# 512-column products for the output projection, the second MLP matrix and the values, with a shared pool of weight buffers

## The chip, the cores and the metric

The kernel runs on one core of one Trainium2 chip. The metric is the device time of one execution in microseconds; each kernel is executed several times and the median is taken. TensorE (PE) multiplies and writes only to PSUM, VectorE (DVE) and ScalarE (ACT) work on SBUF and PSUM, SyncE (SP) starts the transfers, GpSimd (POOL) has little to do here.

## The reference, cut to what matters

Two layers. In each, a mixer with four branches (gated convolution, Conformer convolution module, differential attention, neighbourhood attention) is followed by gates, one output projection and a squared-ReLU MLP. Layer 0 works on 256 latent and 256 context tokens, layer 1 on the 256 latent tokens alone, with keys and values of the context.

```python
glu = p[I_CA] * jax.nn.sigmoid(p[I_CG])
y_b = jax.nn.silu(layer_norm(dwconv(glu, dw, db), lg, lb))       # norm over 512 channels
...
o = jnp.einsum('bhqk,bkhv->bqhv', pd, v)                          # values v: 512 columns per branch
...
y = merge_out(p[I_GATE], (y_a, y_b, y_c, y_d), w_branch[l], b_branch[l], w_o[l])   # merged @ w_o
x = layer_norm(DEEPNORM_ALPHA * x + g1 * y, ln_g[l, 0], ln_b[l, 0])
a = relu(h @ w1); y = (a * a) @ w2                                # w1: 1024 x 4096, w2: 4096 x 1024
x = layer_norm(DEEPNORM_ALPHA * x + g2 * y, ln_g[l, 1], ln_b[l, 1])
```

All numbers are float32. To keep that precision, both operands of a large product are split into a high and a low float32r part, and a product is three matmuls: high by high, high by low, low by high.

## The kernel before, in words

Weights come from memory in units of 128x1024 floats (512 KB): a DMA on SP brings `raw`, ACT rounds it to `whi`, DVE subtracts to `wlo`, PE uses both. `weight_order()` lists the units, `w_load`, `w_hi` and `w_lo` walk down the list, and `weight()` hands the next unit to the main thread. Each of the three stages has three buffers. A further two hold `araw`, the blocks of the adaLN matrix; DVE (and ACT for a few) multiplies these into the running sums `sums`, from which one small matmul makes the modulation row. That work fills the stretches from about 300 to 530 us and from 660 to 950 us.

Every thread of work is a Python generator. A planner (`Sched.run`) knows costs per instruction and a priority per thread, and at each step gives out the instruction that can start first; this sets the order on each engine, and the engines then run those orders with semaphores between them. On PE, the main thread (projections, merge, MLP) and the attention threads interleave in this way.

Projections `in`, `br` and `f1` compute their results with channels on partitions and tokens along the columns (512 columns in layer 0, 256 in layer 1). The value projections (`values`, units `dv` and `nv`), the output projection (`out_proj`, `wo`) and the second MLP matrix (`ff2`, `f2`, shown as `f` in the profile) have 128 tokens on partitions and weights along the columns: 256 columns per PSUM tile, `nb` counting the four column blocks, a unit holding four of the eight 128-row slices of one block. PSUM has eight buffers of one bank; at most four are `main` (projections), four `att` (attention).

`residual` works off a PSUM tile on DVE: a multiplication by the gate row, an addition, a `bn_stats`. `ff2_evac` adds up the four quarters of the MLP in `yacc`. `conv_b_norm` computes the mean (`mu`) and variance (`var`) over 512 channels, which lie in four tiles of 128 partitions, by matmuls with a matrix of constants in float32. In the last layer `blocks` takes the last two column blocks tile by tile, so that the first token tile can be normalised while the second is computed; two units are kept (`held`) for the second pass.

Of the kernel before, what the change touches and what calls it, by code (L numbers as in the profile page):

```python
# [21 lines left out]
N_S = 70  # L22
# [19 lines left out]
MARGIN = 20  # L42
CAPS_PS = {"main": 4, "att": 4, "ada": 1}
# [11 lines left out]
def unit_table():  # L55

    names = []
    for m in range(76):
        if not (M_DV <= m < M_DV + 4 or M_NV <= m < M_NV + 4):
            names.append(("in", m))  # L60
    for br in ("dv", "nv"):
        names += [(br, s, h) for s in range(2) for h in range(2)]
    names += [("br", i, mp) for i in range(4) for mp in range(4)]
    names += [("wo", nb, h) for nb in range(4) for h in range(2)]
    names += [("f1", m) for m in range(32)]
    names += [("f2", qd, nb, h) for qd in range(4) for nb in range(4) for h in range(2)]
    return {n: i for i, n in enumerate(names)}
# [237 lines left out]
class Kernel(Sched):  # L305
    def __init__(self, tc, es, aps):
# [125 lines left out]
    def gemm(self, out, pairs, cost):  # L432

        n = len(pairs)
        step = max(1, int(1300 // (3 * cost)))
        for i in range(0, n, step):
            calls, r = [], []
            for j in range(i, min(n, i + step)):
                a, b = pairs[j]
                calls += self.mm3(out, a, b, j == 0, j == n - 1)  # L440
                r += [a[0], a[1], b[0], b[1]]
            yield self.mm(calls, [out], r, (cost + 2) * len(calls))

# [108 lines left out]
    def w_load(self):  # L552
        for i, (l, name) in enumerate(self.order):
            if i < FIRST:
                yield self.wait("x0", 1, W_AFTER[i])
            raw = yield self.alloc("raw", name="raw")
# [3 lines left out]
    def w_hi(self):  # L560
        for i in range(len(self.order)):
# [6 lines left out]
            else:  # L568
                hi = yield self.alloc("whi", dt=F32R, name="whi", n=1)
# [3 lines left out]
    def w_lo(self):  # L573
        for i in range(len(self.order)):
# [8 lines left out]
            else:  # L583
                lo = yield self.alloc("wlo", dt=F32R, name="wlo", n=1)
# [4 lines left out]
    def weight(self, l, *name):  # L589
# [6 lines left out]
        kn = 128 if name[0] in ("in", "f1") else 256  # L596
        return Weight(w, kn)

    def weights(self, l, name):
        w = []  # L600
        for h in range(2):
            x = yield from self.weight(l, *name, h)
            w.append(x)
        return w

    @staticmethod
    def blocks(l):

        both = (0, 1)
        if l < DEPTH - 1:  # L610
            return [(nb, both) for nb in range(4)]
        return [(0, both), (1, both), (2, (0,)), (3, (0,)), (2, (1,)), (3, (1,))]

    def weight_order(self):
        o = []
        for l in range(DEPTH):
# [5 lines left out]
            def diff(st):  # L622
# [3 lines left out]
                a("dv", st, 0)  # L626
                a("dv", st, 1)

            def na(st):
# [3 lines left out]
                a("nv", st, 0)  # L633
                a("nv", st, 1)
# [19 lines left out]
            for s in range(S):  # L654
                for nb in range(4):
                    a("wo", nb, 0)
                    a("wo", nb, 1)
            f1 = lambda m0, m1: [a("f1", m) for m in range(m0, m1)]
            f2 = lambda qd: [a("f2", qd, nb, h) for nb in range(4) for h in range(2)]
# [10 lines left out]
    def ada(self, l, g, pace):  # L670
# [16 lines left out]
        for k in range(KD):  # L687
            raws = []
            for h in range(2):
                yield self.wait("pace", pace + 2 * k + h)  # L690
                raw = yield self.alloc("araw", name="araw")
# [290 lines left out]
    def conv_b_norm(self, l, n):  # L982
        ys = []
        for ct in range(4):
            y = yield self.wait("conf", l, ct)
            ys.append(y)
        yield self.wait("pace", self.base[l] + NORM_PACE)
        mu = yield self.alloc("ps", "att", name="mu")
        for ct in range(4):
            yield self.ones_mm(mu[:, 0:n], self.on512, ys[ct][:, 0:n], ct == 0, ct == 3)  # L990
        var = yield self.alloc("ps", "att", name="var")
        for ct in range(4):
            z = ys[ct][:, 0:n]
            yield self.tt(z, z, mu[:, 0:n], ALU.subtract)
            sq = yield self.s("tmp", F32, "sq")
# [3 lines left out]
        self.release(mu)  # L999
        r = yield from self.rsqrt(var[:, 0:n], n)  # L1000
# [98 lines left out]
    def values(self, l, br, st, uses):  # L1099

        w = []
        for h in range(2):
            x = yield from self.weight(l, br, st, h)
            w.append(x)
        vs = []
        for i in range(2):
            p = yield from self.pair("qkv", "v")
            vs.append(p)
        left = [4]
        for t in range(4):  # L1110
            ps = yield self.alloc("ps", "main", name="v")
            c = slice(t * 128, t * 128 + 128)
            yield from self.gemm(ps[:, 0:256], [(self.ucut(l, 0, k, c.start, c.stop),
                                                 w[k // 4](k % 4)) for k in range(KD)], 107)
            self.spawn(self.value_split(l, br, st, t, ps, vs, left, uses), 12)
        for x in w:
            self.release(*x.views())

    def value_split(self, l, br, st, t, ps, vs, left, uses):
        vb = yield self.wait("vb", l, br, st)  # L1120
        f = yield self.s("att", F32, "vf")
        yield self.tt(f[:, 0:256], ps[:, 0:256], vb[:, 0:256], ALU.add)
        self.release(ps)
        p = vs[t // 2]
        c = slice((t % 2) * 256, (t % 2) * 256 + 256)
        yield from self.split(f[:, 0:256], p[0][:, c], p[1][:, c])
        self.release(f)
        left[0] -= 1
        if not left[0]:
            self.release(vb)  # L1130
            self.shared((br, l, st), [x for p in vs for x in p], uses)

    def value_bias(self, l, br, st, pace):
# [3 lines left out]
        c0 = (O_DV if br == "dv" else O_NV) + st * 256  # L1137
        yield self.dma(vb[:, 0:256], self.b_row[l:l + 1, c0:c0 + 256].to_broadcast([128, 256]), 1 << 17)
        self.signal("vb", l, br, st, val=vb)
# [15 lines left out]
    def diff_soft(self, l, st, j, s, qt):  # L1155
# [4 lines left out]
        q = yield self.wait("q", l, "d", st, j)  # L1160
        S = yield self.alloc("ps", "att", name="S", n=2)
# [5 lines left out]
        p = yield self.alloc("s", "P", name="P", n=2)  # L1167
# [10 lines left out]
    def na_soft(self, l, st, h, s, qt):  # L1178
# [4 lines left out]
        q = yield self.wait("q", l, "n", st, j)  # L1183
        if s == 0:
# [11 lines left out]
        p = yield self.s("P", F32, "P")  # L1196
# [7 lines left out]
    def p_parts(self, l, kind, h, s):  # L1204
# [7 lines left out]
        for kp in range(nkp):  # L1212
            t = yield self.alloc("ps", "att", name="PT")
# [9 lines left out]
            pt = yield from self.pair("pt", "pt")  # L1223
# [5 lines left out]
    def pv(self, o, vs, c0, pts, s):  # L1229
        pairs = []  # L1230
        for kt in range(2 * len(pts)):
            t = kt + 2 * s
            v = vs[2 * (t // 2):2 * (t // 2) + 2]
            c = slice((t % 2) * 256 + c0, (t % 2) * 256 + c0 + 128)
# [4 lines left out]
    def diff_head(self, l, st, j, n):  # L1239
# [5 lines left out]
        vs = yield self.wait("dv", l, st)  # L1245
        o = yield self.alloc("ps", "att", name="o")
        for s in range(n // 256):
            yield from self.pv(o[:, s * 256:s * 256 + 256], vs, j * 128, pts[s], s)
            for p in pts[s]:
                self.release(*p)  # L1250
        self.done("dv", l, st)
# [14 lines left out]
    def na_head(self, l, st, h, n):  # L1266
# [6 lines left out]
        vs = yield self.wait("nv", l, st)  # L1273
        o = yield self.alloc("ps", "att", name="o")
        for s in range(n // 256):
            yield from self.pv(o[:, s * 256:s * 256 + 256], vs, j * 128, pts[s], s)
            for p in pts[s]:
                self.release(*p)
        self.done("nv", l, st)
# [12 lines left out]
    def diff_stage(self, l, st, n):  # L1292
# [11 lines left out]
        yield from self.values(l, "dv", st, 2)  # L1304

    def na_stage(self, l, st, n):
# [15 lines left out]
        yield from self.values(l, "nv", st, 4)  # L1322
# [67 lines left out]
    def normalise(self, r, stv, gb=None):  # L1390

        nc = self.nc
        st4 = stv[:, 0:24].re("p (c n) -> p c n", n=6)
# [19 lines left out]
    def residual(self, l, j, s, t, cols, ps, r, x, gB, stv, part):  # L1413

        nc = self.nc
        if part is None:
            yield self.tt(r, ps, gB, ALU.mult)
            self.release(ps)
            yield self.stt(r, x, ALPHA, r, ALU.mult, ALU.add)
        else:  # L1420
            f = yield self.s("tmp", F32, "yf")
            yield self.tt(f[:, 0:256], ps, gB, ALU.mult)
            self.release(ps)
            yield self.wait("pre", l, t, cols)
            yield self.tt(r, f[:, 0:256], r, ALU.add)
            self.release(f)
        o = stv[:, cols * 6:cols * 6 + 6]
        yield self.dve(335, lambda: nc.vector.bn_stats(out=o.ap, in_=r.ap), [o], [r])
        self.signal("res", l, j, t, cols)
# [20 lines left out]
    def norm_tile(self, l, j, t, r, stv):  # L1450
# [5 lines left out]
        for nb in range(4):  # L1456
            yield self.wait("res", l, j, t, nb)
# [3 lines left out]
        yield from self.normalise(r, stv, gb)  # L1461
# [23 lines left out]
    def out_proj(self, l, s, merged):  # L1485
# [14 lines left out]
        ws = {}  # L1500
        for nb, which in self.blocks(l):
            if nb not in ws:
                ws[nb] = yield from self.weights(l, ("wo", nb))
            w = ws[nb]
            c = slice((nb % 2) * 256, (nb % 2) * 256 + 256)
            for i in which:
                ps = yield self.alloc("ps", "main", name="wo")
                tk = slice(s * 256 + i * 128, s * 256 + i * 128 + 128)
                yield from self.gemm(ps[:, 0:256], [(self.cut(merged[k], (slice(None), tk)), w[k // 4](k % 4))
                                                    for k in range(KD)], 107)  # L1510
                self.spawn(self.residual(l, 0, s, 2 * s + i, nb, ps[:, 0:256], rs[i][nb // 2][:, c],
                                         xs[i][nb // 2][:, c], gB[nb // 2][:, c], sts[i], None), 2)
            if which[-1] == 1:
                for x in w:
                    self.release(*x.views())
        self.spawn(self.free_rows(("gB", l, 0, s), [("res", l, 0, 2 * s + i, nb) for i in range(2) for nb in range(4)]), 50)
# [53 lines left out]
    def ff2_evac(self, l, qd, t, nb, ps, y):  # L1570
# [5 lines left out]
        if qd == 2:  # L1576
            self.spawn(self.ffn_residual(l, t, nb, y), 55)

    def ffn_residual(self, l, t, nb, y):
# [3 lines left out]
        c = slice((nb % 2) * 256, (nb % 2) * 256 + 256)  # L1583
# [289 lines left out]
```

## Time and profile before

| what | value |
|---|---|
| median of 3 runs | 1643.44 us (1642.19 to 1646.79) |
| profiled execution | 1644.06 us |
| its span | 1642.3 us |
| PE busy | 1604.0 us (98%) |
| DVE busy | 1298.5 us (79%) |
| ACT busy | 884.6 us (54%) |
| moved by DMA | 254.55 MB, mean 155 GB/s |

The profiled execution's time is 1.8 us more than its span, and 0.6 us more than the median. Matmuls overlap in the profile, so the duration of a single one (about 285 ns for 256 columns, 390 ns for 512) says less than the distance between starts in a long stretch, which the chain of waits shows as a time and a count. For the other engines the mean duration of a group can be multiplied by its count.

### The profile page before, as it was taken

What the parts mean: (1) busy time and instruction counts of PE and PEld (TensorE: products, weight loads), DVE (VectorE), ACT (ScalarE), POOL (GpSimd) and SP (SyncE); (2) the same over time, 40 slices, a digit from 0 to 9 for tenths busy, and PEclk for the clock granted to TensorE, in tenths of its full rate; (3) what the DMA queues carried; (4) which work ended last, traced back from release to release, by engine and by line L of the source; (5) the groups of instructions that cost most, each with busy time, mean ns of one, the idle gap of its engine ahead of it and who ended that gap; (6) DMA issues with size and microseconds to landing.
All of it is one profiled execution on the core that took longest, in us unless ns stands there. A gap on an engine that the chain in (4) does not pass through costs nothing.

```text
span 1642.3 us, 26846 instructions
## 1 busy us (share of the span) xinstructions
PE 1604.0 (98%) x10568; PEld 1451.5 (88%) x10568; DVE 1298.5 (79%) x2285; ACT 884.6 (54%) x1444; POOL 11.0 (1%) x51
## 2 busy tenths in 40 slices
PE   7999999999999999999999999998999999989997
PEld 4888888887888889889898889998999999989997
DVE  3899999699999448875877866999999796774566
ACT  3475484556655344642524324665677675466553
POOL 0000000000000000000000000000000000000000
PEclk9999999999999999999999999999999999999999
DMA  9322322553552345455656634634353445636563
GB/s 356 114 81 77 97 74 90 186 189 126 176 172 95 109 148 182 158 192 161 208 175 207 219 98 134 192 115 141 114 163 125 146 133 185 226 129 183 187 218 119
DMA packets 81299, 254.55 MB, mean 155 GB/s; under 512 B 9092, under 2 KB 14980, under 8 KB 81172
## 3 DMA queue, kind: packets, MB, share of 16 engines
q1 hardware_dynamic: 81172, 252.84, 47.5%
q8 instruction: 82, 1.34, 0.3%
q14 instruction: 45, 0.37, 0.1%
HBM read 250.67 MB, written 2.13 MB: 154 GB/s over the span
## 4 chain that ended last, share of the span: by engine, by line
PE 89%; DMA 5%; DVE 4%; ACT 2%; issue 1%; SPq 0%; POOLq 0%; POOL 0%; DVEq 0%; ACTq 0%
PE mm L423 50%; PE f L423 13%; PE br L423 8%; PE v L423 5%; PE wo L423 4%; PE o L423 2%; DMA araw<-in_w_ada 2%; PE S L423 2%; PE PT L449 1%; DVE wlo L376 1%; DMA a<-in_w_ada 1%; DVE sums L403 1%; ACT whi L369 1%; PE ada L423 1%; SPq L414 0%
## 5 line engine op out<-in xcount | busy, mean ns | idle before, releaser
L423 PE MATMUL mm<-u,whi 128*128 128x512 f32 (+1 forms) x3168 | 791.8, 341 | 2.4 <-ACT u L369 1.6
L369 ACT ACTIVATE whi<-raw 128x1024 fp32r<-128x1024 f32 x335 | 354.4, 1059 | 481.5 <-PE mm L423 236.9
L423 PEld LDWEIGHTS mm<-u,whi 128*128 128x128 f32 x3168 | 548.3, 192 | 67.1 <-ACT u L369 2.5
L376 DVE TENSOR_TENSOR wlo<-raw,whi 128x1024 fp32r<-128x1024 f32 x335 | 408.7, 1222 | 198.4 <-ACT whi L369 195.2
L423 PE MATMUL mm<-u,wlo 128*128 128x512 f32 (+1 forms) x1584 | 536.3, 339 | 0.8 <-DVE wlo L376 0.8
L423 PEld LDWEIGHTS mm<-u,wlo 128*128 128x128 f32 x1584 | 303.5, 192 | 32.6 <-DVE wlo L376 1.0
L423 PE MATMUL f<-whi,a 128*128 128x256 f32 x1504 | 276.6, 285 | 0.5 <-ACT a L369 0.2
L423 PEld LDWEIGHTS f<-whi,a 128*128 128x128 f32 x1504 | 237.0, 193 | 3.6 <-issue 2.5
L423 PE MATMUL f<-wlo,a 128*128 128x256 f32 x752 | 213.8, 284 | 2.6 <-DVE wlo L376 2.6
L403 DVE SCALAR_TENSOR_TENSOR sums<-araw,cs,sums 128x512 f32<-128x512 f32 x280 | 194.8, 744 | 25.3 <-DMA araw<-in_w_ada 25.0
L423 PEld LDWEIGHTS f<-wlo,a 128*128 128x128 f32 x752 | 145.0, 193 | 3.4 <-DVE wlo L376 3.2
L403 DVE SCALAR_TENSOR_TENSOR conf<-glu,sm,conf 128x512 f32<-128x512 f32 (+1 forms) x240 | 137.9, 612 | 1.0
L423 PE MATMUL v<-whi,u 128*128 128x256 f32 x512 | 96.7, 283 | 0.3 <-DVE pt L376 0.3
L423 PEld LDWEIGHTS v<-whi,u 128*128 128x128 f32 x512 | 81.6, 191 | 1.5 <-PE S L423 0.7
L423 PE MATMUL v<-wlo,u 128*128 128x256 f32 x256 | 72.4, 283 | 0.0
L369 ACT ACTIVATE P<-S,st 128x512 f32<-128x512 f32 (+1 forms) x96 | 58.4, 612 | 24.0 <-DVE st L1150 23.5
L423 PE MATMUL wo<-whi,mg 128*128 128x256 f32 x352 | 67.3, 289 | 3.1 <-ACT mg L369 2.6
L423 PEld LDWEIGHTS wo<-whi,mg 128*128 128x128 f32 x352 | 56.7, 196 | 4.1 <-ACT mg L369 3.0
L1150 DVE TENSOR_REDUCE st<-S 128x1 f32<-128x512 f32 (+1 forms) x96 | 55.5, 589 | 1.5 <-PE S L423 1.3
L369 ACT ACTIVATE qk<-ra 64x512 fp32r<-64x512 f32 (+1 forms) x74 | 42.8, 578 | 20.2 <-DVE ra L376 18.8
L423 PE MATMUL o<-pt,v 128*128 128x256 f32 x360 | 47.9, 285 | 2.7 <-ACT pt L369 1.4
L423 PE MATMUL wo<-wlo,mg 128*128 128x256 f32 x176 | 50.4, 286 | 0.0
(194 smaller groups left out, 1910.9 us busy)
## 6 DMA issues: line engine op xcount, KB each, us to landing
raw<-in_W SPq DMA_DIRECT2D x344, 512.0 KB
araw<-in_w_ada SPq DMA_DIRECT2D x80, 512.0 KB
a<-in_w_ada SPq DMA_DIRECT2D x32, 256.0 KB
bt<-in_rpb SPq DMA_DIRECT2D x32, 128.0 KB
row<-g SPq DMA_DIRECT2D x12, 256.0 KB
x<-in_x_t SPq DMA_DIRECT2D x8, 256.0 KB
row<-in_ln_g SPq DMA_DIRECT2D x8, 256.0 KB
row<-in_ln_b SPq DMA_DIRECT2D x8, 256.0 KB
```

Of the source, the lines that this page charges most:

```text
L369: lambda: nc.scalar.activation(out=out.ap, in_=in_.ap, func=func, **kw),
L376: return self._op(eng, cost, lambda: e.tensor_tensor(out=out.ap, in0=x.ap, in1=y.ap, op=op), [out], [x, y])
L403: return self._op("DVE", cost, lambda: nc.vector.scalar_tensor_tensor(out=out.ap, in0=x.ap, scalar=a(s), in1=y.ap, op0=op0, op1=op1), [out ...
L423: nc.tensor.matmul(out=out, lhsT=x, rhs=y, start=start, stop=stop, **kw)
L449: nc.tensor.transpose(o.ap, i.ap, ident.ap)
L1150: yield self.dve(68 + 1.04 * nk, lambda: nc.vector.tensor_reduce(out=mx.ap, in_=S.ap, axis=AX.X, op=ALU.max, negate=True), [mx], [S])
```

## The change

The wide products. One function, `wide`, does the value projections, the output projection and the second MLP matrix with 512 columns per PSUM tile. A unit now holds two of the eight row slices of a 512-column block. For each of the four units `q` of a block it goes through all token tiles `i`, adding six matmuls to each tile's PSUM buffer, before it takes the next unit; before, one PSUM tile got all its 24 matmuls in a row. So four PSUM buffers are filled at once where there are four token tiles (layer 0's second MLP matrix but for its last quarter, all values), else two or one.

```diff
+    def wide(self, l, name, nb, which, tiles, a, ws, done):
+        parts = self.parts(l, nb, which, tiles)
+        for c0, cw in parts:
+            ps = {}
+            for q in range(4):
+                if len(ws) <= q:
+                    w = yield from self.weight(l, *name, q)
+                    ws.append(w)
+                w = ws[q]
+                for i in which:
+                    if not q:
+                        ps[i] = yield self.alloc("ps", "main", name=name[0])
+                    tk = slice(i * 128, i * 128 + 128)
+                    yield from self.gemm(ps[i][:, 0:cw], [(self.cut(a[2 * q + k], (slice(None), tk)), w(k, slice(c0, c0 + cw)))
+                                                          for k in range(2)], 0.4167 * cw, q == 0, q == 3)
+                    if q == 3:
+                        done(i, nb * 512 + c0, cw, ps[i])
+                if which[-1] == tiles[-1] and (c0, cw) == parts[-1]:
+                    self.release(*w.views())
+    def parts(l, nb, which, tiles):
+        if l == DEPTH - 1 and nb == 1 and len(tiles) == 2 and which == (tiles[1],):
+            return [(0, 256), (256, 256)]
+        return [(0, 512)]
+    def grain(l, i):
+        return 256 if l == DEPTH - 1 and i == 1 else 512
...
-            return [(nb, both) for nb in range(4)]
-        return [(0, both), (1, both), (2, (0,)), (3, (0,)), (2, (1,)), (3, (1,))]
+            return [(0, (0, 1)), (1, (0, 1))]
+        return [(0, (0, 1)), (1, (0,)), (1, (1,))]
...
-                a("dv", st, 0)
-                a("dv", st, 1)
+                if not st:
+                    for q in range(4):
+                        a("dv", q)
```

In the last layer the last column block of the second token tile stays in two parts of 256. Both halves of a branch's values are now computed in its first attention stage (`nv` as `dv`). `value_split`, `residual` and `ff2_evac` work on 512 columns at a time; `bn_stats` too, except in the last layer's second tile.

At the head of the first output projection, on PE, `wo` are the PSUM tiles, `whi` and `wlo` the weights, `mg` the eight merged slices (each a high tile and a low tile with the next number). The rows of before stand at the change of the unit:

```order
L423 MATMUL wo_5944<-whi_5822,mg_5699 128x256
L423 MATMUL wo_5944<-wlo_5831,mg_5699 128x256
L423 MATMUL wo_5944<-whi_5822,mg_5700 128x256
L423 MATMUL wo_5944<-whi_5860,mg_5771 128x256
L423 MATMUL wo_5944<-wlo_5864,mg_5771 128x256
L423 MATMUL wo_5944<-whi_5860,mg_5772 128x256
```

The same tile goes on with the fifth slice (`mg_5771`) at its thirteenth matmul. The rows of after, on the same engine and place:

```order
L421 MATMUL wo_5708<-whi_5587,mg_5322 128x512
L421 MATMUL wo_5708<-wlo_5595,mg_5322 128x512
L421 MATMUL wo_5708<-whi_5587,mg_5323 128x512
L421 MATMUL wo_5716<-whi_5587,mg_5281 128x512
L421 MATMUL wo_5716<-wlo_5595,mg_5281 128x512
L421 MATMUL wo_5716<-whi_5587,mg_5282 128x512
L421 MATMUL wo_5716<-whi_5587,mg_5322 128x512
L421 MATMUL wo_5716<-wlo_5595,mg_5322 128x512
L421 MATMUL wo_5716<-whi_5587,mg_5323 128x512
L421 MATMUL wo_5708<-whi_5624,mg_5407 128x512
```

After the second slice (`mg_5322`) PE turns to the second token tile (`wo_5716`) with the first two slices, and the third slice comes at the thirteenth matmul of the block; the last two slices come with the fourth unit, after 36 matmuls.

The conv norm. `conv_b_norm` adds the four channel tiles on DVE as they come, and the four squares likewise, and leaves one matmul each for `mu` and `var`; it needs `var`'s PSUM buffer only then.

```diff
+            if ct == 1:
+                sum_ = yield self.s("tmp", F32, "sum")
+                yield self.tt(sum_[:, 0:n], ys[0][:, 0:n], y[:, 0:n], ALU.add)
+            elif ct > 1:
+                yield self.tt(sum_[:, 0:n], sum_[:, 0:n], y[:, 0:n], ALU.add)
...
-        for ct in range(4):
-            yield self.ones_mm(mu[:, 0:n], self.on512, ys[ct][:, 0:n], ct == 0, ct == 3)
+        yield self.ones_mm(mu[:, 0:n], self.on512, sum_[:, 0:n], True, True)
...
+                yield self.act(sum_[:, 0:n], z, AF.Square)
...
-            yield self.ones_mm(var[:, 0:n], self.on512, sq[:, 0:n], ct == 0, ct == 3)
+            yield self.tt(sum_[:, 0:n], sum_[:, 0:n], sq[:, 0:n], ALU.add)
```

On PE in layer 0's merge, before:

```order
L423 MATMUL br<-yc,whi 128x512 x2
L423 MATMUL br<-yc,wlo 128x512
L423 MATMUL mu<-conf,on_77 128x512 x4
L423 MATMUL br<-yc,whi 128x512 x2
L423 MATMUL br<-yc,wlo 128x512
```

and after:

```order
L421 MATMUL br<-yc,whi 128x512 x2
L421 MATMUL br<-yc,wlo 128x512
L421 MATMUL mu<-sum,on_77 128x512
L421 MATMUL mm<-u,whi 128x512 x2
L421 MATMUL mm<-u,wlo 128x512
```

Four matmuls of the mean have become one that reads `sum`; `var` likewise.

The buffers. `raw`, `whi`, `wlo` and `araw` had 3, 3, 3 and 2 buffers of their own. Now all four take from one pool of ten, each up to the same number; the pool of 128x512 tiles grows from 70 to 73. A few allocations of `P` and `pt` come before those of the PSUM tile they are used with.

```diff
-            "raw": Resource(big, "raw", [128, 1024], 3),
-            "whi": Resource(big, "whi", [128, 1024], 3),
-            "wlo": Resource(big, "wlo", [128, 1024], 3),
-            "araw": Resource(big, "araw", [128, 1024], 2),
+            "wt": Resource(big, "wt", [128, 1024], 10, CAPS_W),
```

On SP, in layer 0's MLP, where both kinds of block are loaded (the names after `waits` are the semaphores by engine, DMAHW being transfers). Before:

```order
L414 DMA raw<-in_W 128x1024 [waits DMAHW2_49,DVE_49]
L414 DMA raw<-in_W 128x1024 [waits DMAHW5_49,DVE_49]
L414 DMA araw<-in_w_ada 128x1024 [waits DMAHW7_49]
L414 DMA araw<-in_w_ada 128x1024 [waits DMAHW0_49,DVE_49]
L414 DMA raw<-in_W 128x1024 [waits DMAHW6_49,DVE_49]
```

and after:

```order
L412 DMA raw<-in_W 128x1024 [waits DMAHW4_49,DMAHW2_49,DVE_49]
L412 DMA araw<-in_w_ada 128x1024 [waits PE_49]
L412 DMA raw<-in_W 128x1024 [waits PE_49]
L412 DMA araw<-in_w_ada 128x1024 [waits DMAHW5_49,DMAHW3_49,DVE_49]
L412 DMA raw<-in_W 128x1024 [waits DMAHW0_49,DVE_49]
L412 DMA araw<-in_w_ada 128x1024 [waits DMAHW7_49,PE_49]
```

The loads come one of a kind after the other instead of in pairs, and some wait for PE, which has to finish with a weight buffer, where all waited for DVE or for earlier transfers.

More of the change, by code (lines that the diff above doesn't have):

```diff
@@ L21 @@
 LN_EPS = 1e-5
-N_S = 70
+N_S = 73
 NORM_PACE = 56
@@ L42 @@
 MARGIN = 20
+CAPS_W = {"raw": 3, "whi": 3, "wlo": 3, "araw": 2}
 CAPS_PS = {"main": 4, "att": 4, "ada": 1}
@@ L430, in mm3, with gemm @@
         return [(out.ap, x.ap, y.ap, first and j == 0, last and j == 2, {}) for j, (x, y) in enumerate(o)]
-    def gemm(self, out, pairs, cost):
+    def gemm(self, out, pairs, cost, first=True, last=True):
         n = len(pairs)
@@ L595, in weight @@
         w = yield self.wait("w", i)
-        kn = 128 if name[0] in ("in", "f1") else 256
+        kn = {"in": 128, "f1": 128, "br": 256}.get(name[0], 512)
         return Weight(w, kn)
[L599 to L604, printed above, removed]
     @staticmethod
     def blocks(l):
-        both = (0, 1)
         if l < DEPTH - 1:
-            return [(nb, both) for nb in range(4)]
-        return [(0, both), (1, both), (2, (0,)), (3, (0,)), (2, (1,)), (3, (1,))]
+            return [(0, (0, 1)), (1, (0, 1))]
+        return [(0, (0, 1)), (1, (0,)), (1, (1,))]
     def weight_order(self):
@@ L632, in na @@
                     a("in", M_NQ + 2 * st + j)
-                a("nv", st, 0)
-                a("nv", st, 1)
+                if not st:
+                    for q in range(4):
+                        a("nv", q)
             def mg(i):
@@ L1303, in diff_stage @@
             self.spawn(self.diff_head(l, st, j, n), 15)
-        yield from self.values(l, "dv", st, 2)
+        if not st:
+            yield from self.values(l, "dv", 4)
     def na_stage(self, l, st, n):
@@ L1321, in na_stage @@
                 self.spawn(self.na_head(l, st, h, n), 15)
-        yield from self.values(l, "nv", st, 4)
+        if not st:
+            yield from self.values(l, "nv", 8)
     def merge_evac(self, l, i, m, n, pb):
@@ L1455, in norm_tile @@
             gb = g, b
-        for nb in range(4):
-            yield self.wait("res", l, j, t, nb)
+        ns = 1024 // self.grain(l, t)
+        for n in range(ns):
+            yield self.wait("res", l, j, t, n)
         if gb:
@@ L1499, in out_proj, with done @@
         self.spawn(self.after_attn_norm(l, s, rs), 2)
-        ws = {}
+        def done(t, c0, cw, ps):
+            i, h, c = t - 2 * s, c0 // 512, slice(c0 % 512, c0 % 512 + cw)
+            self.spawn(self.residual(l, 0, s, t, c0, cw, ps, rs[i][h][:, c], xs[i][h][:, c], gB[h][:, c], sts[i], False), 2)
+        ws = [], []
         for nb, which in self.blocks(l):
[L1502 to L1516, printed above, removed]
+            yield from self.wide(l, ("wo", nb), nb, tuple(2 * s + i for i in which), (2 * s, 2 * s + 1), merged, ws[nb], done)
+        self.spawn(self.free_rows(("gB", l, 0, s), [("res", l, 0, 2 * s + i, n) for i in range(2)
+                                                        for n in range(1024 // self.grain(l, 2 * s + i))]), 50)
     def free_rows(self, name, events):
```

177 lines of the change are left out of this document (81 added, 96 removed).

## The prediction

> **What bounds the kernel now.** The page comes first: span, busy shares, the chain by engine.
>
> ```profile
> span 1642.3 us, 26846 instructions
> PE 1604.0 (98%) x10568; PEld 1451.5 (88%) x10568; DVE 1298.5 (79%) x2285; ACT 884.6 (54%) x1444; POOL 11.0 (1%) x51
> PE 89%; DMA 5%; DVE 4%; ACT 2%; issue 1%; SPq 0%; POOLq 0%; POOL 0%; DVEq 0%; ACTq 0%
> ```
>
> PE is busy for all but 38.3 us, and the chain lies on it for 89%. DVE is the next engine, with a fifth of the span free. So time falls if PE gets less to do and nobody makes it wait. What one matmul takes is read from long stretches in the chain in order of time (start, length, what, count).
>
> ```profile
> 369.60 3.43 PE mu L423 x8
> ...
> 375.78 3.43 PE var L423 x8
> ...
> 553.76 10.88 PE mm L423 x48
> ...
> 1294.50 1.73 PE mu L423 x8
> ...
> 1477.74 23.04 PE f L423 x192
> ```
>
> 48 matmuls of 512 columns in 10.88 us are 226.7 ns each; 192 of 256 columns in 23.04 us are 120.0 ns. Two of the small kind cost 240.0 ns, one large 226.7: a part of 13.3 ns belongs to the matmul and not to its columns.
>
> **The wide products.** How many there are stands in the groups of instructions, shapes kept apart (`f` is the second MLP matrix; `wh`, `wl` are kept units).
>
> ```profile
> L423 PE MATMUL f<-whi,a 128*128 128x256 f32 x1504 | 276.6, 285 | 0.5 <-ACT a L369 0.2 <-DVE a L376 0.2
> L423 PE MATMUL f<-wlo,a 128*128 128x256 f32 x752 | 213.8, 284 | 2.6 <-DVE wlo L376 2.6
> L423 PE MATMUL v<-whi,u 128*128 128x256 f32 x512 | 96.7, 283 | 0.3 <-DVE pt L376 0.3
> L423 PE MATMUL v<-wlo,u 128*128 128x256 f32 x256 | 72.4, 283 | 0.0
> L423 PE MATMUL wo<-whi,mg 128*128 128x256 f32 x352 | 67.3, 289 | 3.1 <-ACT mg L369 2.6 <-DVE mg L376 0.5
> L423 PE MATMUL wo<-wlo,mg 128*128 128x256 f32 x176 | 50.4, 286 | 0.0
> L423 PE MATMUL wo<-wh,mg 128*128 128x256 f32 x32 | 6.1, 283 | 0.0
> L423 PE MATMUL f<-wh,a 128*128 128x256 f32 x32 | 6.1, 283 | 0.0
> L423 PE MATMUL wo<-wl,mg 128*128 128x256 f32 x16 | 4.5, 283 | 0.0
> L423 PE MATMUL f<-wl,a 128*128 128x256 f32 x16 | 4.5, 283 | 0.0
> ```
>
> `f` has 2304, the values 768, `wo` 576. Halved, they would be 1824 fewer; but 48 of `f` and 48 of `wo` stay at 256 columns (last layer, second tile), which keeps 24 pairs each. Removed: 1128 + 384 + 264 = 1776 matmuls. At 13.3 ns: 15.0 + 5.1 + 3.5 = 23.7 us, all on PE. I take the whole of it, since the same two pitches hold in both layers wherever nobody waits.
>
> The Trainium skill speaks against this size: "TensorE: Matmul & The Clock Gate", section "Back-to-back issue gap", gives N/2.4 + 2.5 ns at full clock, so 109.2 and 215.8 ns. By it a merged pair would save 2.5 ns, the 1776 pairs 4.4 us in place of 23.7, as an estimate. The rows above have 120.0 and 226.7, and they decide.
>
> **The conv norm.** Eight records are four matmuls: in layer 0 the mean takes 3.43 us and the variance 3.43, in layer 1 the mean 1.73, and the variance as much again by its like shape. Three of four go: 0.75 x (6.86 + 3.46) = 7.7 us off PE. DVE gets six additions per layer, priced by passes of the same kind:
>
> ```profile
> L376 DVE TENSOR_TENSOR acc<-acc,gth 128x512 f32<-128x512 f32 x24 | 16.5, 687 | 0.3
> ...
> L376 DVE TENSOR_TENSOR acc<-acc,gth 128x256 f32<-128x256 f32 x24 | 10.1, 422 | 0.5
> ```
>
> 6 x 0.687 + 6 x 0.422 = 6.7 us. Against that the evacuations of the wide products become cheaper, since two passes of 256 (0.84 us) become one of 512 (0.69), some hundred times in all. DVE ends a few us below today; I cost it at nothing, with its free fifth as cover. If that cover is gone in a stretch, PE cannot use what it saves there (a rival below). The norm's later variance delays `y` of the Conformer branch by three passes, 2.1 us; its merge comes a whole merge later.
>
> **Waits that go.** The timeline marks where PE sat idle; the stretches give the granted clock (PEclk stands before the last two columns).
>
> ```profile
> 617.82 0.39 PE L423 MATMUL wo<-whi,mg 128*128 128x256 f32 x1 [1.71 <-ACT mg L369]
> 618.55 0.51 PE L423 MATMUL wo<-whi,mg 128*128 128x256 f32 x2 [0.22 <-DVE mg L376]
> ```
>
> ```profile
> 929.74 0.58 PE L423 MATMUL f<-wlo,a 128*128 128x256 f32 x1 [1.98 <-DVE wlo L376]
> ```
>
> ```profile
> 1416.54 0.38 PE L423 MATMUL wo<-whi,mg 128*128 128x256 f32 x1 [0.28 <-DVE mg L376]
> 1417.78 0.38 PE L423 MATMUL wo<-whi,mg 128*128 128x256 f32 x1 [0.86 <-ACT mg L369]
> ```
>
> ```profile
> 618.00:623.00 5.00, 4.78 (x26) 4.57 (x27) 2.30 (x5) 1.06 (x1) 0.00 (x0) 0.66 0.70 256
> ...
> 929.00:932.00 3.00, 2.26 (x10) 2.26 (x11) 2.81 (x4) 0.00 (x0) 0.00 (x0) 0.61 0.36 96
> ```
>
> At both heads of the output projection PE waits for the last merged slices. With the new order these are needed after 36 matmuls, 8.2 us into the block instead of inside the first tile's 24 (2.9 us). That removes 1.93 + 1.14 us of idling, and in layer 0 the slow clock behind it: 5 us at 0.66, so 1.7 us. Together 4.8 us, if the four units' `wlo` are there in time. The same rows show that a pause of 2 us is paid nearly twice. The same page of the Trainium skill (Part 1, the clock gate) halves the clock only after an idle window of about 3.4 us; here 1.9 us of idling were enough, so each new pause is priced by the row.
>
> **Waits that come.** Two things get tighter, and the trace of before shows neither. First, a `main` PSUM buffer was needed again three tiles later, 72 x 0.120 = 8.6 us; with four tiles filled at once the first is finished only 18 matmuls before it is needed, 4.1 us. Behind it stand DVE and ACT, which work in order. Second, `araw` loads now wait for weight buffers that PE gives back, on SP's one queue, and `raw` loads stand behind them. What such transfers already cost, by the view of all instructions on `araw` (idle time before them, times), the waits (total, times, longest) and the chain:
>
> ```profile
>   DMA araw<-in_w_ada: 59.1, 26
> ```
>
> ```profile
> DVE sums L403 <- DMA araw<-in_w_ada: 25.0, 13, 4.6
> ```
>
> ```profile
> 667.28 6.97 DMA araw<-in_w_ada
> ```
>
> DVE and ACT lose 59.1 us to them in all, up to 4.6 us at once, which is more than 4.1. While DVE sits there, the `wlo` behind it is late, as at 929.74. Bounds: from nothing (at 929.74 PE lost 1.98 us to all this) to a quarter of the 59.1, 15 us, doubled in the worst case by a slow clock. I take 5 us, nearest to the rows of what these waits cost PE today, about as much as the heads give back. A unit of `f` in layer 0 lasts 48 x 0.120 = 5.8 us on PE today and 24 x 0.2267 = 5.4 us after, so the rate of weights is not the trouble. The tail is left at nothing either way: its last two blocks keep 256 columns.
>
> **The sum.** 23.7 + 7.7 + 4.8 - 5 = 31.2 us. The profiled execution's 1644.06 us become 1612.9; it stands 0.6 us above the median of 1643.44, so 1612 for the median.
>
> **Rivals.** (a) DVE is the bound in the attention stretches.
>
> ```profile
> 328.00:369.00 41.00, 41.00 (x204) 34.75 (x203) 39.54 (x70) 20.28 (x35) 0.00 (x0) 1.00 0.55 189
> ...
> 1220.00:1260.00 40.00, 40.00 (x280) 37.41 (x279) 38.66 (x84) 30.42 (x57) 0.00 (x0) 1.00 0.41 131
> ```
>
> 39.54 of 41 and 38.66 of 40 us (third busy column) leave little; against it, PE was fully busy too, and part of that DVE work has no near deadline. If all that the values and the norm save there is lost (5.1 + 7.7), or new pauses cost 15 us instead of 5, the time is 1622 to 1625. (b) The new order gives more: no new pause, and the wait at 929.74 goes as well (2 us and 1.2 of slow clock): 1612 - 5 - 3 = 1604. (c) The products get no cheaper, because turning among PSUM buffers every six matmuls costs what the merging saves: only the norm is left, 1636. Against it: the 192 matmuls above change buffer eight times without a step. The formula of the Trainium skill's page named above would give 1631, near this case. (d) Slower: the shared pool throttles. If each of the 40 steps of the adaLN work (80 `araw` loads in pairs) made PE wait for its buffer chain, PE return, load, `sums`, `wlo`, by more than 1.0 us, the gain of 36 us before pauses and the margin of 5 are gone; at 1.3 us each the time is 1612 - 5 + 52 = 1659. Today the wait at 929.74 is the one such pause that the rows above show.
>
> **How the numbers follow.** This kernel's runs differ by 0.3%, some 5 us, and less cannot be told from no change. Forecast (1606 to 1618): 0.50. (a), 1618 to 1628: 0.24. (b), below 1606: 0.12. (c), 1628 to 1638: 0.07. No change, by (d) half-way: 0.03. (d): 0.04. The range 1602 to 1628 holds the forecast, (a) and most of (b). Faster: 0.93.
>
> **What would show it.** Right: `f`, `dv`, `nv` and `wo` stand at 1128, 384 and 264 matmuls of 512 columns, `f` at 226.7 ns in long stretches; PE busy near 1604 - 31 = 1573 us; `mu` and `var` two records each per layer; no idling on `mg` at the heads of `wo`. Wrong: `f` stretches above 230 ns; PE idle in 700 to 950 us, released by `wlo` or an evacuation, with `araw` waits of DVE well over 59 us; or PE idle in 1060 to 1260 us with DVE full.

## The result, and the profile after

The changed kernel takes 1604.79 us (median of 4 runs, 1603.61 to 1606.23); the kernel before 1642.82 us (median of 4 runs, 1640.66 to 1646.79). The ratio is 0.9766, with a 95% interval from 0.9745 to 0.9788. That is 38 us less, where the sum said 31: inside the range, but 7 us below the forecast, at the time of rival (b).

The page of the profiled execution (1606.23 us): span, then busy time, share and instructions of each engine.

```profile
span 1604.5 us, 23073 instructions
PE 1571.9 (98%) x8768; PEld 1349.3 (84%) x8768; DVE 1290.1 (80%) x2156; ACT 883.2 (55%) x1413; POOL 12.0 (1%) x51
```

PE's busy time fell by 32.1 us (1573 was forecast), its idle time from 38.3 to 32.6 us. DVE ended 8 us lower. The groups of matmuls have the counts that the prediction gave:

```profile
L421 PE MATMUL f<-whi,a 128*128 128x512 f32 x744 | 232.1, 390 | 0.0
L421 PE MATMUL f<-wlo,a 128*128 128x512 f32 x372 | 145.0, 390 | 0.0
L421 PE MATMUL wo<-whi,mg 128*128 128x512 f32 x168 | 53.1, 391 | 0.0
L421 PE MATMUL dv<-whi,u 128*128 128x512 f32 x128 | 43.4, 397 | 0.0
L421 PE MATMUL mu<-sum,on 128*128 128x512 f32 x2 | 1.0, 592 | 0.0
```

The last column, the idle time before the group, is the news: `f` and `wo` wait for nothing any more (before, `f` waited 2.6 us on `wlo` and `wo` 3.1 us on `mg`). From the chain (start, length, what, count):

```profile
1272.59 0.43 PE mu L421 x2
...
1384.59 22.11 PE wo L421 x120
...
1444.83 21.79 PE f L421 x96
```

96 wide matmuls in 21.79 us are 227.0 ns each. The 120 of `wo` are 72 wide and 48 narrow, 72 x 226.7 + 48 x 120.0 = 22.08 us: in layer 1 the output projection runs without a gap. The timeline (idle time before a row in brackets) shows new gaps instead:

```profile
754.47 3.35 PE L421 MATMUL ada<-sums,ones 128*32 128x512 f32 x16
757.75 0.51 PE L421 MATMUL f<-whi,a 128*128 128x512 f32 x1
```

```profile
937.99 1.91 PE L421 MATMUL ada<-sums,ones 128*32 128x512 f32 x10
940.94 1.05 PE L421 MATMUL ada<-sums,ones 128*32 128x512 f32 x4 [1.05 <-DVE sums L401]
942.21 1.04 PE L421 MATMUL ada<-sums,ones 128*32 128x512 f32 x2 [0.21 <-DVE sums L401]
943.18 0.74 PE L421 MATMUL mm<-u,whi 128*128 128x512 f32 x2
```

```profile
1299.35 0.33 PE L481 MATMUL PT<-ident,P 128*128 128x128 f32 x1 [3.08 <-ACT P L367]
1301.78 0.90 PE L481 MATMUL PT<-ident,P 128*128 128x128 f32 x3 [2.10 <-ACT P L367]
```

In the kernel before, the last step of an adaLN group stands in the same view like this:

```profile
404.39 1.94 PE L423 MATMUL ada<-sums,ones 128*32 128x512 f32 x16
406.26 0.51 PE L423 MATMUL S<-qk 128*128 128x256 f32 x2
```

From its start to the next one it takes 1.87 us. At 754 us of the changed kernel it takes 3.28 us and at 938 us 5.19: PE stands there for DVE's `sums`, 4.7 us in all, most of it hidden in what counts as busy. And PE waits 5.2 us for the softmax at 1299. The stretches around that, with the granted clock third from the end:

```profile
1290.00:1300.00 10.00, 6.60 (x41) 5.61 (x39) 9.50 (x20) 9.61 (x20) 0.00 (x0) 1.00 0.47 154
1300.00:1310.00 10.00, 8.22 (x41) 7.45 (x42) 9.29 (x27) 8.81 (x19) 0.00 (x0) 0.66 0.06 19
```

10 us at 0.66 cost up to 3.4 us more. So pauses did come, and more than the 5 us of the sum. The experiments had to find what paid for them.

### The profile page after: what moved, and what is told of

Same layout as the page of the kernel before. It is cut to its first block, busy times and chain, and to the rows that moved or that the text cites. A ratio compares the mean times of both kernels' runs of the same rounds, so it can differ in the third digit from the quotient of the medians.

```text
span 1604.5 us, 23073 instructions
## 1 busy us (share of the span) xinstructions
PE 1571.9 (98%) x8768; PEld 1349.3 (84%) x8768; DVE 1290.1 (80%) x2156; ACT 883.2 (55%) x1413; POOL 12.0 (1%) x51
## 5 line engine op out<-in xcount | busy, mean ns | idle before, releaser
L421 PEld LDWEIGHTS mm<-u,wlo 128*128 128x128 f32 x1584 | 301.4, 190 | 32.3 <-DVE wlo L374 0.6
L421 PE MATMUL f<-whi,a 128*128 128x512 f32 (+1 forms) x760 | 235.3, 388 | 0.0
L421 PEld LDWEIGHTS f<-whi,a 128*128 128x128 f32 x760 | 142.3, 188 | 29.5 <-issue 0.8
L421 PE MATMUL f<-wlo,a 128*128 128x512 f32 (+1 forms) x380 | 147.2, 387 | 0.0
L421 PEld LDWEIGHTS f<-wlo,a 128*128 128x128 f32 x380 | 71.4, 188 | 14.5 <-DVE wlo L374 0.2
L367 ACT ACTIVATE gth<-mm,hb 128x512 f32<-128x512 f32 (+1 forms) x64 | 36.9, 577 | 42.5 <-PE mm L421 42.2
L421 PE MATMUL wo<-whi,mg 128*128 128x512 f32 (+1 forms) x184 | 56.3, 382 | 0.0
L367 ACT ACTIVATE bh<-br,hb 128x512 f32<-128x512 f32 (+1 forms) x64 | 36.4, 573 | 27.0 <-PE br L421 26.9
L367 ACT ACTIVATE a2f<-mm 128x512 f32<-128x512 f32 (+1 forms) x64 | 30.8, 482 | 33.1 <-PE mm L421 33.0
L421 PE MATMUL S<-qk 128*128 128x512 f32 (+1 forms) x192 | 47.8, 369 | 1.0 <-ACT P L367 0.7
L421 PEld LDWEIGHTS o<-pt,v 128*128 128x128 f32 x360 | 45.4, 191 | 1.6 <-issue 0.5
```

The source lines that it names most:

```text
L367: lambda: nc.scalar.activation(out=out.ap, in_=in_.ap, func=func, **kw),
L421: nc.tensor.matmul(out=out, lhsT=x, rhs=y, start=start, stop=stop, **kw)
```

## Experiments: what a merged product is worth

**Two halves for each wide matmul.** The order, the buffers and the waits stay; only the count goes back.

```diff
-calls += self.mm3(out, a, b, ...)            # 512 columns
+for c in (0, 256):
+    calls += self.mm3(out[:, c:c+256], a, [x[:, c:c+256] for x in b], ...)
```

> The changed kernel, but each matmul of 512 columns in the second MLP matrix, the values and the output projection is issued as two of 256 columns next to each other (same stationary operand, same PSUM buffer, and the order of everything else as it is). 1776 matmuls more. Theory (a matmul costs 13.3 ns beside its columns, PE is the bound): 1604.8 + 1776 x 0.0133 = 1628.4 us, between 1627 and 1630. Rival by the formula of the Trainium skill, 'TensorE: Matmul & The Clock Gate', 'Back-to-back issue gap' (2.5 ns): 1604.8 + 4.4 = 1609.2 us. Rival that the gain came from the order of the work and not from the count: 1605 us, and then the count is worth nothing.

Measured: 1622.18 us, ratio to the kernel before 0.9877 [0.9863, 0.9891]. That is 17.4 us more than the changed kernel, between the 1628.4 us of the theory and the 1609.2 us of the formula. The chain of this kernel:

```profile
1455.70 23.04 PE f L422 x192
```

120.0 ns each, so a pair costs 240 ns against 227: the 13 ns are there. Most of what is missing is at the adaLN steps. With halves, PE comes to them later, and in the timeline all five stand as they should, at 760 us for instance:

```profile
759.98 1.94 PE L422 MATMUL ada<-sums,ones 128*32 128x512 f32 x16
```

So the wide products save more than 17.4 us on PE, and 4 to 5 of it turn into a new wait for `sums`. Against the kernel below in which these steps come later (1600.70 us), the halves are 21.5 us slower, 12.1 ns for each of 1776 matmuls; the last 2.2 us to the 23.7 of the sum stay open. The pause on `P` near 1300 us stands in all three kernels and drops out of the comparison. The formula of the Trainium skill ("TensorE: Matmul & The Clock Gate", "Back-to-back issue gap"), which that section calls the isolated gap, would have given 1609 us; the runs exclude it as the distance between these matmuls.

**Quarters.** The same with 128 columns.

> The changed kernel with each wide matmul of 512 columns issued as four of 128 next to each other, everything else in its order: 5328 matmuls more. Theory (13.3 ns for each matmul beside its columns, at any width): a matmul of 128 columns takes 66.7 ns, 1604.8 + 5328 x 0.0133 = 1676 us. Rival (a matmul can't be shorter than the load of its stationary operand, which PE does beside the matmul before it; nothing in the traces shows that bound, and 120 ns is an upper one): at 100 ns each, 1776 x (400 - 226.7) ns = 308 us more, 1913 us. By the Trainium skill's formula ('TensorE: Matmul & The Clock Gate', 'Back-to-back issue gap') 128 columns take 55.8 ns, and 2.5 x 5328 ns = 13 us would be added, 1618 us.

Measured: 1995.15 us, ratio 1.2144 [1.2128, 1.2161], 390 us more than the changed kernel.

```profile
926.62 85.71 PE f L422 x768
```

111.6 ns each, where 66.7 would follow from 13.3 ns and the columns. 1776 x (4 x 111.6 - 226.7) ns is 390 us, all of the difference. So 13.3 ns per matmul is no law: it holds from 512 to 256 columns, and at 128 the time is far above it. That reads like a floor of some 110 ns, but no other width was run. The Trainium skill's section "LDWEIGHTS (loading the stationary operand)" on the same page gives columns / 1.2, so 106.7 ns for 128 columns of the stationary operand; the row agrees within 5 ns, though no run here varied the load by itself. The loads' own records last 186 to 192 ns in this trace, longer than the 111.6 ns from one to the next, so they overlap and do not settle it.

## Experiments: which part brought what

Two kernels lead from the kernel before to the changed one, the pool alone and the pool with the new norm; two more test the pool. The shared pool (10 buffers, caps as in the change) replaces the four separate groups of weight buffers; `N_S` is the number of small buffers.

```diff
 shared pool alone, 73 small buffers:
-"raw": Resource(..., 3), "whi": ..., 3, "wlo": ..., 3, "araw": ..., 2
+"wt": Resource(big, "wt", [128, 1024], 10, CAPS_W)
-N_S = 70
+N_S = 73
 then with the conv norm: conv_b_norm as in the change
 pool with the old count: N_S = 70
 separate buffers, one small buffer more: N_S = 71
```

> The kernel before with one change: raw, whi, wlo and araw draw on one pool of 10 buffers with the caps of the changed kernel (and 73 small buffers in place of 70). Theory: the pool is worth nothing by itself, PE stays as busy as before: 1643 us, within 3 us. Rival 1, it throttles (the prediction's case d): slower by 5 us or more, with the waits on the araw loads well over 59 us. Rival 2, it is where the 6 us beyond the prediction came from: 1637 us.

> The kernel before with the shared pool and the new conv norm (sums of the channel tiles on DVE), all products as before. Theory: 7.7 us less on PE than with the shared pool alone, so 1643 - 7.7 = 1635.3 us if the pool is worth nothing. Rival, DVE has no room for the six additions in these stretches: less than 4 us comes, 1639 us or more.

> The kernel before with the shared pool of 10 weight buffers, but with its own 70 small buffers. The shared pool with 73 small buffers took 1629.0 us where the kernel before took 1642.3. Theory: the pool itself does it, since a load takes whichever weight buffer comes free first: 1629 to 1632 us here too. Rival: it is the three more small buffers that the saved weight buffer pays for, through which the planner starts rows and attention steps earlier: 1640 to 1643 us here.

> The kernel before with separate weight buffers as it has them and 71 small buffers in place of 70 (no more fit). It tells whether any change of the count moves the planner's order, and the pauses with it. If the pool does it: 1642 us, within 3. If the small buffers do it: a third of 13.3 us or more, 1638 us or less. If the pauses of the kernel before are an accident of one order among many: anything between 1629 and 1642 us, with other pauses of PE in other places than before.

| kernel | us | ratio to before, 95% interval | idle on `araw` loads, us |
|---|---|---|---|
| separate buffers, 71 small | 1644.75 | 1.0016 [1.0006, 1.0025] | 55.1 |
| pool, 70 small | 1639.55 | 0.9984 [0.9974, 0.9994] | 31.9 |
| pool, 73 small | 1628.97 | 0.9916 [0.9902, 0.9931] | 32.3 |
| pool, 73 small, new norm | 1623.56 | 0.9886 [0.9870, 0.9902] | 33.0 |
| changed kernel | 1604.79 | 0.9766 [0.9745, 0.9788] | 56.2 |

The last column is the idle time of DVE and ACT that ended with such a load (59.1 us in the kernel before). The pool with its three small buffers is worth 13.3 us, which no term of the prediction held as a gain, and which the first expectation missed too. In the changed kernel the idle time in the last column is back at 56.2 us, and the pauses of PE that the pool took out stay away: the column measures DVE and ACT, and is not itself the gain. With 70 small buffers most of the pauses of the kernel before are gone already; as an example the stretch of 1120 to 1140 us, of the kernel before and then of the pool with 70:

```profile
1120.00:1140.00 20.00, 15.64 (x101) 14.62 (x101) 18.17 (x42) 12.48 (x17) 0.13 (x2) 0.83 0.25 79
```

```profile
1120.00:1140.00 20.00, 18.85 (x153) 18.21 (x152) 19.69 (x41) 14.29 (x21) 0.13 (x2) 1.00 0.34 107
```

But that kernel has one large pause which none of the others has, and which eats the gain:

```profile
448.34 5.47 DVE L401 SCALAR_TENSOR_TENSOR sums<-araw,cs,sums 128x512 f32<-128x512 f32 x8
456.22 0.90 PE L447 MATMUL PT<-ident,P 128*128 128x128 f32 x3 [9.27 <-ACT P L367]
```

DVE is busy all the while: eight `sums` passes in a row and two `wlo` stand in its order ahead of the small step that the softmax needs. The stretch behind it, with the clock again third from the end:

```profile
457.00:467.00 10.00, 10.00 (x71) 9.48 (x71) 8.41 (x27) 9.03 (x23) 0.00 (x0) 0.88 0.28 94
```

With 73 it is not there, and the time is 10.6 us less: 9.27 and 1.2 of slow clock. Whether 70 buffers force this order, or it is one accident among many, was not tried. One small buffer more without the pool does nothing of the kind (2 us slower), and its waits on `araw` stay at 55 us.

The pool also works where the prediction looked to the new order of the output projection. With the pool and 73 small buffers, and the old order, the group that waited 3.1 us on `mg` stands like this:

```profile
L421 PE MATMUL wo<-whi,mg 128*128 128x256 f32 x352 | 65.7, 285 | 0.9 <-ACT mg L367 0.6 <-DVE mg L374 0.2
```

The 10 us from this kernel's head in layer 0 on (612 to 622 us) have a clock of 1.00, so the slow clock behind that head is gone too.

Why the pool halves the waits on `araw` is seen in what SP's queue waits for before it issues a load (total, times, longest). Of the kernel before:

```profile
SPq L414 <- DVE wlo L376: 840.4, 200, 14.2
```

and of the pool with 70 small buffers:

```profile
SPq L412 <- PE mm L421: 675.9, 176, 14.7
SPq L412 <- DVE wlo L374: 115.3, 70, 6.9
```

With separate buffers a `raw` load takes the buffer that DVE has just read for `wlo`; the `araw` load behind it in the queue waits too, and DVE waits for that `araw` load: a loop through DVE. The pool gives out the buffer that has been free longest, mostly one that PE finished with. That the waits fall with the pool alone is shown; that this loop is the reason is read from the rows and the code, and no run separates it.

The new norm takes 6.0 us off PE's busy time in the page (1596.8 to 1590.8) and 5.4 us off the time, not 7.7. In layer 0 the timeline has new pauses, the first two of four (2.5 us in all from 507 to 542 us, against one of 0.5 without the norm):

```profile
507.51 1.94 PE L421 MATMUL ada<-sums,ones 128*32 128x512 f32 x16 [0.65 <-ACT gth L367]
...
536.23 0.55 PE L447 MATMUL PT<-ident,P 128*128 128x128 f32 x3 [1.05 <-ACT P L367]
```

The wait of `f` for `wlo` near 910 us also grew, from 0.88 to 1.81 us. Whether the additions on DVE cause this or only the new order was not tried. The last step, all wide products together with the values in the first stage and the earlier allocations of `P` and `pt`, brings 18.8 us.

## Experiments: the heads of the output projection

```diff
-..., merged, ws[nb], done)
+..., [merged[k] for k in (6, 7, 4, 5, 2, 3, 0, 1)], ws[nb], done)
```

> The changed kernel, but the output projection takes the merged slices in the order 6, 7, 4, 5, 2, 3, 0, 1 (the weight units are laid out to match), so the last merged slices are needed at once and not after 36 matmuls. Theory (the head of the output projection waited in the kernel before, because the slices were needed 2.9 us into the block): now PE waits for them in full, 1.93 + 2.9 us in layer 0 and 1.14 + 2.9 us in layer 1, 8.9 us, with some 2 to 4 us of slow clock behind them: 1604.8 + 11 to 13 = 1616 to 1618 us. Rival, the merges finish with room anyway, since the work ahead was moved as well: 1605 us, and the 4.8 us of the prediction came from elsewhere.

Measured: 1611.24 us, ratio 0.9808 [0.9793, 0.9823], 6.5 us slower than the changed kernel. The timeline at the two heads (layer 0, layer 1):

```profile
609.61 0.80 PE L421 MATMUL wo<-whi,mg 128*128 128x512 f32 x1 [2.46 <-ACT mg L367]
```

```profile
1389.86 0.50 PE L421 MATMUL wo<-whi,mg 128*128 128x512 f32 x1 [1.87 <-ACT mg L367]
```

The stretches from these heads on:

```profile
609.00:619.00 10.00, 9.39 (x35) 7.64 (x36) 3.47 (x4) 3.62 (x4) 0.00 (x0) 0.83 0.67 227
1389.00:1399.00 10.00, 9.14 (x33) 7.31 (x34) 5.64 (x8) 4.50 (x7) 0.00 (x0) 0.83 0.55 195
```

The pauses come back where they were expected, at half the size: 4.3 us of idling, and twice 10 us at 0.83, 3.4 us at most. In the changed kernel itself the head of layer 0 and the writing of the last slice stand so:

```profile
607.65 0.39 PE L421 MATMUL wo<-whi,mg 128*128 128x512 f32 x1
610.94 0.69 DVE L374 TENSOR_TENSOR mg<-acc,mg 128x512 fp32r<-128x512 f32 x1 [0.70 <-ACT mg L367]
```

So the last slice is there 4.0 us after the head in layer 0, and 3.2 us after it in layer 1 (1384.43 and 1387.60 us), 4 to 5 us ahead of the 8.2 us at which it is needed. The mechanism holds; that PE waited 1.93 us before, 2.9 us into the block, does not carry over as a date, since the merges ahead were replanned as well.

## Experiments: the pauses that came

**The adaLN steps later.**

```diff
         if sums:
+            if l:
+                yield self.wait("pace", pace + 2 * KD + 4)
             ps = yield self.alloc("ps", "ada", name="ada")
```

> The changed kernel, with the last step of each adaLN group of layer 1 (eight matmuls that add up the sums) put four weight units later in the order. In the changed kernel PE stands at two of these steps, at 754 and at 938 us, until DVE has the sums: 3.28 and 5.19 us for what takes 1.87 us elsewhere, 4.7 us together. Theory (the wide products bring PE to these steps earlier than the araw loads allow): they go, 1604.8 - 4.7 = 1600 us. Rival, the loads are late all the same and the pause moves to the next product that waits for wlo behind them on DVE: 1604 us or more.

Measured: 1600.70 us, ratio 0.9743 [0.9730, 0.9756], 4.1 us less. The timeline has the last of these steps at its usual length:

```profile
944.59 1.94 PE L421 MATMUL ada<-sums,ones 128*32 128x512 f32 x16
```

PE had arrived too early, and no other wait took the place of this one.

**The norm of layer 1 later.**

```diff
-yield self.wait("pace", self.base[l] + NORM_PACE)
+yield self.wait("pace", self.base[l] + (NORM_PACE, 67)[l])
```

> The changed kernel, with the conv norm of layer 1 put later by 11 weight units of its pace (67 in place of 56), which moves it some 20 us of PE's work back. In the changed kernel PE waits 5.2 us for P of the softmax at 1299 and 1302 us, and 10 us at 0.66 of the clock stand there, with DVE busy for 9.50 and ACT for 9.61 of the 10 us before 1300. Theory (a): the norm's passes fill DVE and ACT just there, since the values of the second stage no longer stand between its heads: 5.2 + 3.4 us go, 1596 us. Rival: the softmax is late without the norm too, or the merge after it now waits for y: 1604 us or more.

Measured: 1617.39 us, ratio 0.9845 [0.9831, 0.9858], 12.6 us slower, where the theory said 1596 us. Of the 5.2 us of waiting for `P`, 2.3 us are there without the norm (1297 to 1299 us), so the norm has a part in that pause; but PE then waits for `var` (1.69 us), `o`, `PT` and `br` up to 1326 us. Its stretch of 40 us, then that of the changed kernel:

```profile
1290.00:1330.00 40.00, 28.16 (x169) 23.37 (x168) 31.65 (x74) 29.91 (x63) 0.00 (x0) 0.91 0.14 45
```

```profile
1290.00:1330.00 40.00, 34.83 (x251) 33.06 (x250) 33.60 (x71) 33.75 (x67) 0.00 (x0) 0.91 0.30 100
```

DVE is busy for 31.65 us where it was 33.60: less crowded, and PE still waits more. A crowded DVE alone does not explain the pause; the next experiment changes what PE has to do meanwhile.

**The values as they were**, 256 columns, the second stage's between the second stage's heads; first in both layers, then the same with the late adaLN steps, then with the late steps and in layer 1 alone.

```diff
-        if not st:
-            yield from self.values(l, "nv", 8)      # 512 columns, all heads
+        yield from self.values(l, "nv", st, 4)      # 256 columns, this stage's heads
 (the same for "dv"; in the third kernel where l == DEPTH - 1)
```

> The changed kernel with the values as they were: 256 columns at a time, the second stage's values between the second stage's heads. The second MLP matrix and the output projection stay wide, and the pool, the small buffers and the norm are those of the changed kernel. 384 matmuls more, 5.1 us. Theory (a pause paid for part of the values' gain: with their matmuls moved ahead, PE has less to do between the heads of the second stage, and waits 5.2 us for P at 1299 and 1302 us, with some 3 us of slow clock): 1604.8 + 5.1 - 8.6 = 1601 us, and no idling on P after 1280 us. Rival, the pause has another cause (the norm's passes on DVE and ACT, which stay): 1610 us, with the pause.

> As the one before, with the last steps of the adaLN groups of layer 1 four weight units later, which by itself took the changed kernel from 1604.8 to 1600.7 us. Theory: both pauses go, 1601 - 4 = 1597 us, under every kernel so far. Rival (the pause at 1299 us has another cause): 1606 us.

> The kernel with the late adaLN steps (1600.7 us) and the values of layer 1 alone as they were (256 columns, the second stage's between its heads); layer 0 keeps the wide ones. With the values as they were in both layers the stretch from 1290 to 1320 us lost 2.3 us of PE at full clock where the wide ones lose 5.0 to 5.2 us and 3.4 us of slow clock, but layer 0 waited 3.9 us more for P at 532 to 543 us, which the wide ones don't, and 1.1 us more at 1106 us. Theory (the pause belongs to the wide values of layer 1): 1600.7 + 192 x 0.0133 - 6.3 + 1.1 = 1598 us. Rival, the pauses come from the planner's order as a whole and appear elsewhere: 1601 us or more.

Measured: 1609.45 us (ratio 0.9797 [0.9783, 0.9812]), 1606.31 us (0.9775 [0.9762, 0.9788]) and 1597.54 us (0.9725 [0.9710, 0.9740]). In both layers the rival seemed right, 4.7 us more for 384 matmuls; but the trace shows two effects that cancel. In the first of these kernels layer 1 loses 2.3 us near 1300, at full clock (the stretch), and layer 0 has new waits for P (the timeline):

```profile
1290.00:1330.00 40.00, 37.69 (x306) 36.70 (x305) 35.29 (x75) 30.38 (x65) 0.00 (x0) 1.00 0.36 110
```

```profile
531.96 0.55 PE L481 MATMUL PT<-ident,P 128*128 128x128 f32 x3 [1.53 <-ACT P L367]
541.88 0.30 PE L481 MATMUL PT<-ident,P 128*128 128x128 f32 x1 [1.46 <-DVE P L381]
543.11 0.55 PE L481 MATMUL PT<-ident,P 128*128 128x128 f32 x3 [0.93 <-DVE P L381]
```

With the narrow values in layer 1 alone, 1598 us was expected and 1597.54 measured, 3.2 us under the kernel with late adaLN steps although it has 192 matmuls more. Its stretch around the old pause, and what is left of the pause in the timeline:

```profile
1285.00:1325.00 40.00, 37.71 (x307) 36.73 (x306) 32.50 (x68) 28.43 (x58) 0.00 (x0) 1.00 0.30 97
```

```profile
1297.06 0.38 PE L421 MATMUL br<-yb,whi 128*128 128x256 f32 x1 [1.41 <-ACT yb L367]
1297.87 0.39 PE L421 MATMUL br<-yb,whi 128*128 128x256 f32 x1 [0.43 <-DVE yb L374]
1300.81 0.55 PE L481 MATMUL PT<-ident,P 128*128 128x128 f32 x3 [0.45 <-ACT P L367]
```

So that pause is the price of the wide values in layer 1, 3.4 us of slow clock with it: their matmuls no longer stand between the heads of the second stage, where PE waits on DVE and ACT. This is the fastest kernel here, 45 us under the kernel before.

## Why the prediction was right or wrong, point by point

- **What bounds the kernel.** Right: PE is busy for 98% before and after, and every part that made PE's work less or its pauses fewer moved the time.
- **Wide products, 23.7 us.** Right in mechanism and nearly in size: 227.0 ns in long stretches, counts as given, 12.1 ns per matmul in the comparison free of the adaLN pause (21.5 us). The 2.5 ns of the Trainium skill's formula was rightly set aside: by it the halves would have cost 4.4 us, and they cost 17.4.
- **Conv norm, 7.7 us.** A little too large: 5.4 us. The step in doubt is "I cost it at nothing, with its free fifth as cover": DVE's free fifth is an average over the span, and 2 us of new pauses stood in the attention of layer 0 with the new norm.
- **Waits that go, 4.8 us at the heads of `wo`.** Right that they go, and that the order can do it: no gap is left, and taking the last slices first brings 4.3 us of waiting back, with 6.5 us of time. But the order is not what took most of them here. With the pool alone and the old order, the 3.1 us of waiting on `mg` are 0.9 us and the 1.7 us of slow clock are gone, so about 3.9 of the 4.8 us came with the pool.
- **Waits that come, 5 us.** The term that was mis-sized, twice over. What came was about twice as much: 4.1 us at the adaLN steps and, in layer 1's values, 3.2 us net of 192 matmuls x 13.3 ns = 2.6 us, so 5.8 us; together 9.9 us. Of the two causes that it named, the PSUM buffers cost nothing: no row of `f`, `wo`, `dv` or `nv` waits for an evacuation. The second, "`araw` loads now wait for weight buffers that PE gives back", was priced as a cost, and the pool with its small buffers gave 13.3 us instead: the heads of `wo`, most of 929.74 (0.88 us are left), and pauses that the prediction did not list, as at 1120 to 1140 us. The prediction also has the longest single wait too short: 4.6 us is DVE's, and ACT waited 7.2 us for one `araw` load before.
- **The sum.** Luck has a part in it. A gain that no term held (13.3 us, less the 3.9 us at the heads that the sum had) and losses larger than their terms (9.9 us for 5, and 2.3 us less from the norm) partly cancelled, and the time fell inside the range. The steps of 13.3 and 5.4 us are measured, so only the last step tests the terms: 23.7 + 0.9 - 9.9 = 14.7 us, against 18.8 measured. The kernel with pool and norm has some 5.4 us of waits where the changed kernel has none (2.5 us from 507 to 542 us, 1.81 near 910, 0.68 and 0.47 near 1117), which would fill the difference. That the wide products removed them is read from the timelines, and no run separates it.
- **Rivals.** (b) has the time, not the reason: pauses came, and older ones went by more. (a) is real in one place, 5.8 us in layer 1's second stage, but in the 1060 to 1260 us that were named PE never sat idle for more than 0.3 us at once. (c) is excluded by the halves. (d), the throttling pool, had the sign wrong: alone it is faster, and in the changed kernel the two adaLN steps are the only places in 700 to 950 us where PE stands for `sums`.

## What to carry to other kernels

In a kernel that one engine bounds at 98%, a merged instruction is worth its fixed part times the count, but only where the engine does not then arrive early at something that a load or a slower engine still has to finish: look up the waits just behind each shortened stretch, and move those steps later. When matmuls are moved ahead of the place where they covered another engine's work, count what cover is left there. A change in which buffer a load is given, with the small buffers that it frees, can be worth more than half of what the arithmetic saves (13.3 us and 23.7 here): read from the DMA queue's waits which engine releases it, and whether that engine itself waits for the queue.

## What the runs showed of the hardware

- A matmul with a new stationary operand of 128 x 128 took 226.7 to 227.0 ns at 512 columns, 120.0 at 256 and 111.6 at 128: from 512 to 256 it falls nearly with the columns, from 256 to 128 hardly.
- A wait inside a group of matmuls can count as busy: 16 matmuls that need 1.87 us stood as 3.35 us of busy PE with no idle time shown. The length of a row against that of its equals tells it.
- Pauses of 2 to 5 us can cost more than their length: 5.2 us of idling at 1299 us was followed by 10 us at a clock of 0.66, and 1.87 us at 1390 us (last slices first) by 10 us at 0.83. A wait of 1.81 us near 910 us (pool and norm) left it at 1.00, and so did three waits of 1.4, 0.4 and 0.5 us within 4 us of each other. The 3.3 us that PE lost among the matmuls of the adaLN step at 938 us left it at 1.00 too.
